# Later transposes of the rotated heads and the merged tiles, and gate rows summed over partitions as two float32r products

## The chip, the cores and the metric

The kernel runs on one core of a Trainium2 chip. The metric is device time in microseconds of one execution; of several executions the median is given. The engines are named as in the profile: PE (TensorE), DVE (VectorE), ACT (ScalarE), POOL (GpSimd) and SP (SyncE, which here only issues weight loads).

## The reference, cut to what matters

One layer of a decoder trunk, 256 tokens, width 2048. A conditioning vector `c` gives six modulation rows (shift, scale and gate, twice). The mixer projects the modulated input to linear-attention heads, sparse-attention heads with a partial rotary, an indexer and two merge gates; both branches are projected, gated, summed and projected again. The channel part is a SwiGLU.

```python
mod = jax.nn.silu(c) @ w_ada[layer] + b_ada[layer]
sh1, sc1, g1, sh2, sc2, g2 = [m[:, None, :] for m in jnp.split(mod, N_MOD, axis=-1)]
h = rms_norm(x, norm1_gain[layer]) * (1.0 + sc1) + sh1
x = x + g1 * hybrid_mixer(h, ...)
h = rms_norm(x, norm2_gain[layer]) * (1.0 + sc2) + sh2
x = x + g2 * swiglu(h, w_gate_up, w_down)
...
q_b = partial_rope(d_q.reshape(B, S, DSA_HEADS, DSA_HEAD_DIM), positions)
k_b = partial_rope(d_k.reshape(B, S, DSA_HEADS, DSA_HEAD_DIM), positions)
...
merged = jax.nn.sigmoid(gate_a) * y_a + jax.nn.sigmoid(gate_b) * y_b
return merged @ w_merge_out
```

The change touches how `q_b`, `k_b` and `merged` are turned so that their channels lie on partitions, and how the two gate rows `g1` and `g2` are summed.

## The kernel before

**The main stream.** Every large product is a list of chunks (`Mm`). A chunk is four rows of 128 weights by 512 columns. ACT rounds the weights to float32r (`hi`, line 311), DVE subtracts (`lo`, line 313), and PE makes three products for each of four rows and each half of the tokens (lines 351 to 353): 24 products of 128x512 per chunk, without a pause between chunks unless something waits. `hi` and `lo` have four buffers of half a chunk each, so ACT can round the halves of chunk i+2 only as PE is done with the halves of chunk i; `run()` (line 368) writes the program in that order: the products of chunk i, then the split of chunk i+2 (`pres`), then, at a group's last chunk, the group's evacuation, and then one step each of three side threads.

**Side threads.** `qa` (linear attention), `qb` (rotary, transposes, gate rows) and `qc` (indexer, sparse attention) are generators. One step's instructions stand between two chunks on PE, and behind the chunk's split on ACT and DVE. A step yields a cost; a thread steps only while the credit that chunks give lasts. `qb.drain` and `qc.drain` run steps at once where a result is needed. All engines are in-order, and the order is that in which the program is written.

**Rotated heads.** When a group of four heads is projected, `qk_evac` (line 926) copies it to `tm`, and `qk_transposes` (line 938) rotates it: `rope` puts six instructions on POOL (lines 784 to 789). Two empty steps later four transposes (line 949) go to PE, and ACT or DVE copies the result to `fA` or `fB` (line 951); a second half follows a step later. `attend(g)` (line 965) reads these at line 978.

**Merged tiles.** `y_b_evac` (line 1040) makes the merged tile `mm` with four DVE instructions (lines 1044 and 1045). `m_transposes` (line 1064) has one empty step, then two halves of four transposes (line 1055) with a cast on ACT (1060) and a subtraction on DVE (1061).

**Gate rows.** DVE gathers silu(c) times the weights per partition in `acc` (line 285). `reduce_rows` (line 902) sums `acc` over partitions: a float32 product of a matrix of ones with 512 columns of `acc`, and an addition on DVE. `g1_rows` (line 1130) does four such pieces, one per step, at the start of the merge projection; `g2_rows` (line 1264) at the start of the first down projection. `merge_evac(n)` and `down_evac(n)` first run `qb` until piece n is done.

**Buffers.** Small PE results rotate through three PSUM buffers `pa` (`psum_aux`), the main stream's through four, `pm`. The tile `tm` has one buffer.

Of the kernel before, what the change touches and what calls it, by code (L numbers as in the profile page):

```python
# [7 lines left out]
F32 = mybir.dt.float32  # L8
F32R = mybir.dt.float32r
I32 = mybir.dt.int32  # L10
AF = mybir.ActivationFunctionType
ALU = mybir.AluOpType
# [96 lines left out]
def tile_layer(tc, x, c, positions, norm1_gain, norm2_gain, w_ada, b_ada, w_in, gate_up, gate_bias,  # L109
               gla_gain, w_gla, w_dsa, w_merge, w_ffn_up, w_ffn_down, final_gain, cst, out):  # L110
    nc = tc.nc
    pe, act, dve, pool, sp = nc.tensor, nc.scalar, nc.vector, nc.gpsimd, nc.sync
    with (
# [11 lines left out]
        def name(s):  # L125
            serial[0] += 1
            return f"{s}_{serial[0]}"
# [4 lines left out]
        def psum_aux():  # L132
            return pp.tile([128, 512], F32, tag="pa", bufs=3, name=name("pa"))
# [7 lines left out]
        def parts8(tag):  # L141
            return g8(tag, F32R, (128, 8, S))
# [4 lines left out]
        def work(tag, bufs, shape, dt=F32):  # L147
            return wp.tile(list(shape), dt, tag=tag, bufs=bufs, name=name(tag))

        def t4(tag):  # L150
            return work(tag, 4 if tag == "mm" else 1, [128, 2, 512])
# [5 lines left out]
        cc = cp.tile([128, 528], F32, name="cc")  # L157
# [15 lines left out]
        posi = cp.tile([128, 2], I32, name="posi")  # L173
        act.dma_start(posi, positions.rearrange("(t p) -> p t", p=128), allow_slow_non_contiguous=True)

        ones = cp.tile([128, 128], F32, name="ones")
        pool.memset(ones, 1.0)
        half = cp.tile([128, 2], F32, name="half")
        pool.memset(half, -0.5)
        sc = cp.tile([128, 16], F32, name="sc")  # L180
# [595 lines left out]
        def rope(v, nh, dh, rot, step):  # L776

            hf = rot // 2
            vt = v.rearrange("p t (h e) -> p t h e", e=dh)
            a, b = vt[:, :, :, 0:hf], vt[:, :, :, hf:rot]  # L780
            co, si = (w[:, :, ::step].unsqueeze(2).to_broadcast([128, 2, nh, hf]) for w in (cos, sin))
            tmp = work("rp", 1, [128, 2, 128])
            u, w = (tmp[:, i, 0:2 * nh * hf].rearrange("p (t h e) -> p t h e", t=2, h=nh) for i in range(2))
            pool.tensor_tensor(u, a, si, ALU.mult)  # L784
            pool.tensor_tensor(w, b, si, ALU.mult)
            pool.tensor_tensor(a, a, co, ALU.mult)
            pool.tensor_tensor(a, a, w, ALU.subtract)
            pool.tensor_tensor(b, b, co, ALU.mult)
            pool.tensor_tensor(b, b, u, ALU.add)

        ikw = cp.tile([128, 2, 72], F32, name="ikw")
        bias = cp.tile([128, 384], F32, name="bias")
# [85 lines left out]
        accs = {}  # L878
# [20 lines left out]
            act.dma_start(t, row.unsqueeze(0).to_broadcast([128, D]))  # L899
            return t  # L900

        def reduce_rows(dst, n):

            o = slice(n * 512, (n + 1) * 512)
            ps = psum_aux()
            pe.matmul(ps, ones, accs["t"][:, o], start=True, stop=True)  # L906
            dve.tensor_tensor(dst[:, o], dst[:, o], ps, ALU.add)

        for i, seg in enumerate((4, 3, 2, 5)):
            for j in range(16):  # L910
# [15 lines left out]
        def qk_evac(which, g):  # L926
            def f(ps):
                qb.drain()
                tm = t4("tm")
                for t in range(2):  # L930
                    if which == 0:
                        act.mul(tm[:, t], ps[t], 128 ** -0.5)  # L932
                    else:
                        dve.tensor_copy(tm[:, t], ps[t])
                qb.add(qk_transposes(which, g, tm))
            return f

        def qk_transposes(which, g, tm):
            rope(tm, 4, 128, 32, 1)
            yield 0.2  # L940
            yield 0.2
            qc.drain(lambda: done_heads[0] >= g * 4)
            dst = t4("fB" if which else "fA").rearrange("p a b -> p (a b)")
            heads[g, which] = dst
            for i in range(2):
                ps = psum_aux()
                for a in range(2):
                    for t in range(2):
                        pe.transpose(ps[:, a * S + t * 128:a * S + t * 128 + 128],  # L949
                                     tm[:, t, (i * 2 + a) * 128:(i * 2 + a + 1) * 128], ident)  # L950
                (act.copy if i else dve.tensor_copy)(dst[:, i * 512:(i + 1) * 512], ps)
                yield 0.4
# [87 lines left out]
        def y_b_evac(n):  # L1040
            def f(ps):
                sg = state["sg"]
                for t in range(2):
                    dve.tensor_tensor(sg[:, t], sg[:, t], ps[t], ALU.mult)
                    dve.tensor_tensor(mm[n][:, t], mm[n][:, t], sg[:, t], ALU.add)
                qb.add(m_transposes(n))
            return f

        def split_transposes(src, kt0, dst):

            for i in range(2):
                ps = psum_aux()
                for a in range(2):
                    for t in range(2):
                        pe.transpose(ps[:, a * S + t * 128:a * S + t * 128 + 128],  # L1055
                                     src[:, t, (i * 2 + a) * 128:(i * 2 + a + 1) * 128], ident)
                kt = kt0 + i * 2
                hi = dst[kt // 8][:, kt % 8:kt % 8 + 2, :].rearrange("p a t -> p (a t)")
                lo = dst[2 + kt // 8][:, kt % 8:kt % 8 + 2, :].rearrange("p a t -> p (a t)")
                act.copy(hi, ps)  # L1060
                dve.tensor_sub(lo, ps, hi.bitcast(F32))
                yield 0.7

        def m_transposes(n):
            if n == 0:
                for i in range(4):
                    mT[i] = parts8("gA" if i < 2 else "gB")
            yield
            for cost in split_transposes(mm[n], n * 4, mT):
                state["mT"] = state.get("mT", 0) + 2  # L1070
                yield cost
# [17 lines left out]
        late = {}  # L1089

        def merge_start():
            for t in range(2):
                x1[t] = g8(("gC", "gD")[t])
                act.dma_start(x1[t], x[t * 128:(t + 1) * 128, :])
            late["h2"] = hpair()
            late["g1"] = bcast_row("gr", b_ada[2 * D:3 * D])
            late["g1_done"] = 0
            qb.add(g1_rows())
# [29 lines left out]
            qn.step()  # L1128

        def g1_rows():  # L1130
            for n in range(4):
                reduce_rows(late["g1"], n)
                late["g1_done"] = n + 1
                yield 0.7

        def need_m(kt, t):
            if kt >= 12:
# [124 lines left out]
            act.dma_start(late["fg"], final_gain.unsqueeze(0).to_broadcast([128, D]))  # L1262

        def g2_rows():
            for n in range(4):
                reduce_rows(late["g2"], n)
                late["g2_done"] = n + 1
                yield 0.7

        def down_token(n, t, ps, last):  # L1270
            c = slice(n * 512, (n + 1) * 512)
# [40 lines left out]
        for p, (g0, ng) in enumerate(FF_PARTS):  # L1312
            ex = spread(0) if p == 0 else None
            at_first = len(items)
            for n in range(ng):
                if p == 0 and n == 1:
                    items.append(Call(g2_start))
                for which in range(2):
                    add_group(w_ffn_up, which * DFF + (g0 + n) * 512, 512,
                              Grp(act_h2, up_evac(which, n, n * 4), need_h2), extra=ex if n else None)  # L1320
            if p == 0:
                by_token(at_first)
                items[at_first].ahead = AHEAD - 1
                items[at_first].home = (lambda: g8("gr", F32R), free_acc)
                items.append(Call(lambda: qb.add(g2_rows())))

            def need(kt, t, k0=g0 * 4, top=ng * 4 - 4):
                if kt - k0 >= top:
                    qb.drain(lambda: late["ready"] > kt - k0)
            for n in range(4):  # L1330
                add_group(w_ffn_down, n * 512, 512,
                          Grp(lambda kt, k0=g0 * 4: act_ff(kt - k0), down_evac(n, p == 2), need), g0 * 4, ng * 4)
# [45 lines left out]
```

## Time and profile before

| | |
|---|---|
| median of 3 runs | 1880.08 us (1878.12 to 1884.08) |
| the profiled execution | 1886.39 us, its span 1883.5 us |
| PE busy | 1834.3 us, 97% of the span |
| DVE, ACT, POOL busy | 1286.3, 852.2, 115.8 us |
| the chain that ended last | 88% PE, 84% in lines 351 to 353 |
| mean granted TensorE clock | 0.993 of full |

The trace's rows are read as follows: a start in microseconds from the span's start, a duration, the engine, the line, what is written and read, a count where rows are merged, and in brackets how long the engine had been idle and what ended that. A PE product is pipelined: its row is longer than the distance to the next one's start, so costs on PE are read from starts.

### The profile page before, as it was taken

The numbers are of one execution on the slowest core, as the hardware profiler recorded it, in microseconds if no ns is written. First come the engines' busy times: TensorE is split into PE (matmuls) and PEld (weight loads), VectorE is DVE, ScalarE is ACT, GpSimd is POOL, SyncE is SP. The second block draws the span as 40 slices with busy tenths as digits, with TensorE's granted clock in tenths as the row PEclk, the third lists the DMA queues.
The fourth block names the chain that finished last, engine by engine and source line by source line (L and its number), as shares of the span: only waits on it lengthen the run. The fifth ranks groups of instructions, "written<-read, shape, count | busy, mean of one in ns | idle before, by whom it ended". The sixth has DMA issues, their size and how long they took to land.

```text
span 1883.5 us, 23110 instructions
## 1 busy us (share of the span) xinstructions
PE 1834.3 (97%) x9132; PEld 1508.9 (80%) x9132; DVE 1286.3 (68%) x1441; ACT 852.2 (45%) x1114; POOL 115.8 (6%) x141
## 2 busy tenths in 40 slices
PE   3999999999999999999999999999999999999998
PEld 3888888877788888788887787888788888888886
DVE  6899875898765678777777656677555544554455
ACT  4554444655645444344433446444334444334443
POOL 0000000533210000200000000000000000000002
PEclk8999999999999999999999999999999999999999
DMA  9999853644455888878888754899565555555553
GB/s 369 386 348 317 282 158 105 201 136 153 139 162 172 280 301 291 289 254 293 312 304 309 270 197 160 324 323 314 179 200 193 187 191 188 190 191 195 185 180 133
DMA packets 198077, 440.89 MB, mean 234 GB/s; under 512 B 7832, under 2 KB 14128, under 8 KB 188880
## 3 DMA queue, kind: packets, MB, share of 16 engines
q1 hardware_dynamic: 196544, 433.69, 67.1%
q10 hardware_dynamic: 1424, 5.72, 0.8%
q8 instruction: 71, 1.16, 0.2%
q14 instruction: 38, 0.31, 0.0%
HBM read 437.29 MB, written 2.10 MB: 233 GB/s over the span
## 4 chain that ended last, share of the span: by engine, by line
PE 88%; DVE 5%; DMA 2%; issue 2%; ACT 2%; POOL 1%; SPq 0%; ACTq 0%; POOLq 0%; DVEq 0%
PE pm L351 28%; PE pm L352 28%; PE pm L353 28%; DVE lo L313 2%; DVE acc L285 1%; DMA raw<-in_w_in_dram 1%; ACT hi L311 1%; PE pa L1055 1%; DMA raw<-in_w_branch_dsa_dram 1%; PE pa L978 0%; DVE acc L679 0%; PE pa L949 0%; PE pa L1001 0%; DMA raw<-in_w_ada_dram 0%; PE pa L906 0%
## 5 line engine op out<-in xcount | busy, mean ns | idle before, releaser
L313 DVE TENSOR_TENSOR lo<-raw,hi 128x1024 fp32r<-128x1024 f32 (+1 forms) x630 | 764.8, 1225 | 527.8 <-ACT hi L311 527.3
L311 ACT CAST hi<-raw 128x1024 fp32r<-128x1024 f32 (+1 forms) x630 | 650.4, 1043 | 899.7 <-PE pm L353 690.8
L351 PE MATMUL pm<-hi,h 128*128 128x512 f32 (+1 forms) x1784 | 699.4, 392 | 2.2 <-ACT h L470 1.9
L353 PE MATMUL pm<-hi,h 128*128 128x512 f32 (+1 forms) x1784 | 690.7, 387 | 0.0
L352 PE MATMUL pm<-lo,h 128*128 128x512 f32 (+1 forms) x1784 | 690.2, 387 | 0.2 <-DVE lo L313 0.2
L351 PEld LDWEIGHTS pm<-hi,h 128*128 128x128 f32 x1784 | 336.2, 188 | 70.7 <-ACT h L470 2.3
L353 PEld LDWEIGHTS pm<-hi,h 128*128 128x128 f32 x1784 | 335.9, 188 | 68.8 <-DVE h L477 0.2
L352 PEld LDWEIGHTS pm<-lo,h 128*128 128x128 f32 x1784 | 336.2, 188 | 66.3 <-DVE lo L313 0.7
L351 PE MATMUL pm<-hi,gA 128*128 128x512 f32 x608 | 241.9, 398 | 0.0
L352 PE MATMUL pm<-lo,gA 128*128 128x512 f32 x608 | 236.8, 389 | 0.2 <-DVE lo L313 0.2
L353 PE MATMUL pm<-hi,gB 128*128 128x512 f32 x608 | 236.9, 390 | 0.0
L285 DVE SCALAR_TENSOR_TENSOR acc<-raw,sc,acc 128x2048 f32<-128x2048 f32 (+2 forms) x122 | 218.2, 1790 | 7.6 <-DMA raw<-in_w_ada_dram 6.7
L352 PEld LDWEIGHTS pm<-lo,gA 128*128 128x128 f32 x608 | 114.2, 188 | 25.5 <-issue 1.4
L351 PEld LDWEIGHTS pm<-hi,gA 128*128 128x128 f32 x608 | 114.2, 188 | 24.8 <-issue 1.9
L353 PEld LDWEIGHTS pm<-hi,gB 128*128 128x128 f32 x608 | 114.1, 188 | 23.7
L1279 POOL TENSOR_TENSOR gC<-gC,gr 128x512 f32<-128x512 f32 x3 | 4.9, 1647 | 716.6 <-ACT pm L1277 716.6
L670 POOL TENSOR_TENSOR acc<-gC 128x512 f32<-128x512 f32 x32 | 39.2, 1235 | 38.5 <-DVE acc L679 38.1
L679 DVE TENSOR_TENSOR acc<-gB,acc 128x256 f32<-128x256 f32 x64 | 31.2, 548 | 6.9 <-ACT acc L674 6.8
L986 ACT ACTIVATE S<-S,mx 128x128 f32<-128x128 f32 (+1 forms) x32 | 14.3, 448 | 32.8 <-DVE mx L984 32.8
L784 POOL TENSOR_TENSOR rp<-tm,sin 128x128 f32<-128x128 f32 x9 | 8.3, 921 | 308.6 <-ACT tm L932 183.8
L674 ACT ACTIVATE acc<-acc 128x256 f32<-128x256 f32 x64 | 22.2, 415 | 6.9 <-POOL acc L670 6.7
L351 PE MATMUL pm<-hi,gr 128*128 128x512 f32 x64 | 24.9, 389 | 0.0
(271 smaller groups left out, 1041.3 us busy)
## 6 DMA issues: line engine op xcount, KB each, us to landing
raw<-in_w_in_dram SPq DMA_DIRECT2D x129, 1024.0 KB, 5.1
raw<-in_w_ffn_gate_up_dram SPq DMA_DIRECT2D x88, 1024.0 KB, 5.1
raw<-in_w_ada_dram SPq DMA_DIRECT2D x64, 1024.0 KB, 5.0
raw<-in_w_ffn_down_dram SPq DMA_DIRECT2D x44, 1024.0 KB, 5.1
raw<-in_w_ada_dram SPq DMA_DIRECT2D x64, 512.0 KB, 8.6
raw<-in_w_branch_gla_dram SPq DMA_DIRECT2D x16, 1024.0 KB, 5.2
raw<-in_w_branch_dsa_dram SPq DMA_DIRECT2D x16, 1024.0 KB, 5.2
raw<-in_w_merge_out_dram SPq DMA_DIRECT2D x16, 1024.0 KB, 5.3
```

Of the source, the lines that this page charges most:

```text
L285: dve.scalar_tensor_tensor(a[:, g], it.raw[:, j, g], s, a[:, g], ALU.mult, ALU.add)
L311: act.copy(hv, src)
L313: rests.append(lambda lv=lv, src=src, hv=hv: dve.tensor_sub(lv, src, hv.bitcast(F32)))
L351: pe.matmul(o, a, hv, start=it.first and k == 0, stop=False)
L352: pe.matmul(o, a, lv, start=False, stop=False)
L353: pe.matmul(o, b, hv, start=False, stop=it.last and k == it.nk - 1)
L670: pool.tensor_tensor(d, v, v[:, :, s - 1:s].to_broadcast([128, n, 2 * s]), ALU.subtract)
L674: act.activation(d, d, AF.Exp, scale=(1.0 if u else -1.0) / 16)
L679: dve.tensor_tensor(w, src, d, ALU.mult)
L784: pool.tensor_tensor(u, a, si, ALU.mult)
L986: act.activation(nst[:, a:b], nst[:, a:b], AF.Exp, bias=mx[:, t:t + 1], accum_out=sm[:, t:t + 1])
L1055: pe.transpose(ps[:, a * S + t * 128:a * S + t * 128 + 128], src[:, t, (i * 2 + a) * 128:(i * 2 + a + 1) * 128], ident)
```

## The change

1. `qk_transposes` has a third empty step, `m_transposes` a second one. The transposes of every rotated group and of every merged tile stand one chunk later on PE.
2. `reduce_rows` becomes a generator over the four pieces. For each piece ACT rounds 512 columns of `acc` to float32r (`hv`) and DVE subtracts (`lv`), into the single buffer of `tm`; a step later PE multiplies ones with `hv` and with `lv`, and DVE adds the sum. The rounding of the next piece stands in the same step behind that addition.
3. `ones` becomes float32r, written at the start by an ACT activation (0 times the constants plus 1) that stands ahead of the activation that makes silu(c); POOL's memset goes.

```diff
-        ones = cp.tile([128, 128], F32, name="ones")
-        pool.memset(ones, 1.0)
+        ones = cp.tile([128, 128], F32R, name="ones")
+        act.activation(ones, cc[:, 0:128], AF.Identity, bias=1.0, scale=0.0)
...
-        def reduce_rows(dst, n):
-
-            o = slice(n * 512, (n + 1) * 512)
-            ps = psum_aux()
-            pe.matmul(ps, ones, accs["t"][:, o], start=True, stop=True)
-            dve.tensor_tensor(dst[:, o], dst[:, o], ps, ALU.add)
+        def reduce_rows(dst, done):
+
+            for n in range(4):
+                o = slice(n * 512, (n + 1) * 512)
+                both = work("tm", 1, [128, 2, 512], F32R)
+                hv, lv = both[:, 0], both[:, 1]
+                act.copy(hv, accs["t"][:, o])
+                dve.tensor_sub(lv, accs["t"][:, o], hv.bitcast(F32))
+                yield 0.7
+                ps = psum_aux()
+                pe.matmul(ps, ones, hv, start=True, stop=False)
+                pe.matmul(ps, ones, lv, start=False, stop=True)
+                dve.tensor_tensor(dst[:, o], dst[:, o], ps, ALU.add)
+                late[done] = n + 1
...
             rope(tm, 4, 128, 32, 1)
             yield 0.2
             yield 0.2
+            yield 0.1
             qc.drain(lambda: done_heads[0] >= g * 4)
...
             yield
+            yield
             for cost in split_transposes(mm[n], n * 4, mT):
...
         def g1_rows():
-            for n in range(4):
-                reduce_rows(late["g1"], n)
-                late["g1_done"] = n + 1
-                yield 0.7
+            yield from reduce_rows(late["g1"], "g1_done")
...
         def g2_rows():
-            for n in range(4):
-                reduce_rows(late["g2"], n)
-                late["g2_done"] = n + 1
-                yield 0.7
+            yield from reduce_rows(late["g2"], "g2_done")
```

Three places show how instructions move. The first is PE at the transposes of the last rotated keys (`tm_6616`, group 3). Before, they stand ahead of the chunk whose first weights are `hi_6653`:

```order
L353 MATMUL pm_6627<-hi_6608,h_105 128x512
L949 MATMUL pa_6700<-cc,tm_6616 128x128 x4
L351 MATMUL pm_6626<-hi_6653,h_105 128x512
L352 MATMUL pm_6626<-lo_6654,h_105 128x512
L353 MATMUL pm_6626<-hi_6653,h_105 128x512
```

With the change they stand behind that chunk:

```order
L351 MATMUL pm_6627<-hi_6657,h_105 128x512
L352 MATMUL pm_6627<-lo_6658,h_105 128x512
L353 MATMUL pm_6627<-hi_6657,h_105 128x512
L958 MATMUL pa_6737<-cc,tm_6616 128x128 x4
L351 MATMUL pm_6626<-hi_6689,h_105 128x512
```

So 24 products have come between the copy to `tm_6616` and its transposes.

The second place is PE at the end of the linear attention: the last two tiles of its output are turned (line 760), and the first logits of the sparse attention follow (line 978; 987 with the change). Before, from the second half of the first keys' transposes (`pa_4944`) on:

```order
L949 MATMUL pa_4944<-cc,tm_4763 128x128 x4
...
L760 MATMUL pa_4987<-cc,gr_111 128x128
...
L760 MATMUL pa_4996<-cc,gr_111 128x128
...
L978 MATMUL pa_5006<-fB_4885,fA_4668 128x128
L978 MATMUL pa_5006<-fB_4885,fA_4668 128x256
L351 MATMUL pm_5017<-hi_4916,h_105 128x512
```

With the change:

```order
L760 MATMUL pa_4981<-cc,gr_111 128x128
...
L760 MATMUL pa_4990<-cc,gr_111 128x128
...
L958 MATMUL pa_4999<-cc,tm_4763 128x128 x4
L987 MATMUL pa_5006<-fB_4937,fA_4716 128x128
L987 MATMUL pa_5006<-fB_4937,fA_4716 128x256
L351 MATMUL pm_5017<-hi_4909,h_105 128x512
```

Four `pa` tiles now stand between two chunks, where three did; `pa_5006` takes the buffer of `pa_4981`, where it took that of `pa_4944`, used a chunk earlier.

The third place is the start of the merge projection, on PE and DVE. Before, the first piece of the row stands on PE between the third and the fourth chunk of the group (and each further piece behind one more chunk):

```order
L353 MATMUL pm_8460<-hi_8489,gB_7486 128x512
L906 MATMUL pa_8577<-acc_7538,ones 128x512
L351 MATMUL pm_8459<-hi_8526,gA_7484 128x512
L352 MATMUL pm_8459<-lo_8527,gA_7484 128x512
L353 MATMUL pm_8459<-hi_8526,gB_7486 128x512
```

With the change, on PE, behind the group's fourth chunk:

```order
L353 MATMUL pm_8460<-hi_8523,gB_7486 128x512
L912 MATMUL pa_8614<-tm_8611,ones 128x512
L913 MATMUL pa_8614<-tm_8611,ones 128x512
L912 MATMUL pa_8628<-tm_8618,ones 128x512
L913 MATMUL pa_8628<-tm_8618,ones 128x512
L351 MATMUL pm_8635<-hi_8560,gA_7483 128x512
```

and on DVE, from the split of the chunk after next on:

```order
L313 TENSOR_TENSOR lo_8606<-raw_8493,hi_8605 128x1024
L909 TENSOR_TENSOR tm_8611<-acc_7538,tm_8611 128x512
L914 TENSOR_TENSOR gr_8457<-gr_8457,pa_8614 128x512
L909 TENSOR_TENSOR tm_8618<-acc_7538,tm_8618 128x512
L1116 TENSOR_TENSOR fC_8621<-gr_8457,pm_8459 128x512
```

The first two pieces stand back to back, a chunk later than the first one did: the evacuation of group 0 needs piece 0, and the ordinary step behind it brings piece 1. On ACT the roundings `tm_8611` and `tm_8618` stand one behind the other, behind the rounding of `hi_8605`. At the down projection the same pair stands on PE behind the fourth chunk, but there the rounding of piece 0 stands a chunk ahead of its products; that of piece 1 stands as here.

## Rows read from the trace of the kernel before

**Rows 1.** The page's first part: busy time of each engine, its share of the span, its instructions.

```profile
PE 1834.3 (97%) x9132; PEld 1508.9 (80%) x9132; DVE 1286.3 (68%) x1441; ACT 852.2 (45%) x1114; POOL 115.8 (6%) x141
```

**Rows 2.** The waits of PE over the whole span: who was waited for, then total us, times, the longest.

```profile
PE pa L949 <- POOL tm L789: 3.8, 1, 3.8
PE pa L1161 <- DVE mm L1156: 2.2, 4, 0.9
...
PE pa L1055 <- DVE mm L1045: 1.6, 2, 0.9
```

**Rows 3.** The timeline of PE around the transposes of the last rotated keys, and around their second half. Between the rows of 797.67 and 802.94 stand 12 more products, one start behind the other.

```profile
792.68 0.39 PE L353 MATMUL pm<-hi,h 128*128 128x512 f32 x1
796.91 1.12 PE L949 MATMUL pa<-cc,tm 128*128 128x128 f32 x4 [3.84 <-POOL tm L789]
797.67 0.78 PE L351 MATMUL pm<-hi,h 128*128 128x512 f32 x1
...
802.51 0.63 PE L353 MATMUL pm<-hi,h 128*128 128x512 f32 x1
802.94 0.44 PE L351 MATMUL pm<-hi,h 128*128 128x512 f32 x1
...
805.74 0.60 PE L949 MATMUL pa<-cc,tm 128*128 128x128 f32 x4
...
806.41 0.39 PE L352 MATMUL pm<-lo,h 128*128 128x512 f32 x1
```

**Rows 4.** The timeline of POOL: the last instruction of that group's rotary.

```profile
796.40 0.45 POOL L789 TENSOR_TENSOR tm<-tm,rp 128x128 f32<-128x128 f32 x1
```

**Rows 5.** Two stretches by windows: PE busy (instructions), PEld, DVE, ACT, POOL, then the granted clock, the busy share of the DMA engines and GB/s.

```profile
800.00:802.00 2.00, 2.00 (x6) 1.61 (x5) 1.01 (x1) 0.00 (x0) 0.00 (x0) 0.50 0.06 25
1138.00:1142.00 4.00, 2.31 (x12) 1.43 (x11) 2.82 (x5) 1.77 (x4) 0.82 (x2) 1.00 0.54 208
```

**Rows 6.** The timeline of PE: the transposes of one merged tile that wait.

```profile
1002.71 0.30 PE L1055 MATMUL pa<-cc,mm 128*128 128x128 f32 x1 [0.64 <-DVE mm L1045]
1003.94 0.55 PE L1055 MATMUL pa<-cc,mm 128*128 128x128 f32 x3 [0.93 <-DVE mm L1045]
```

**Rows 7.** The timeline of PE: a piece of a gate row (line 906; a float32 product is two instructions) between products of the main stream.

```profile
1060.01 0.40 PE L353 MATMUL pm<-hi,gB 128*128 128x512 f32 x1
1060.24 1.02 PE L906 MATMUL pa<-acc,ones 128*128 128x512 f32 x2
...
1061.33 0.40 PE L352 MATMUL pm<-lo,gA 128*128 128x512 f32 x1
```

**Rows 8.** The timelines of ACT (the first two rows and the fourth), PE (the third) and DVE (the rest): ACT's order behind a split, and the end of the merge projection's first group.

```profile
1054.52 1.05 ACT L311 CAST hi<-raw 128x1024 fp32r<-128x1024 f32 x1 [1.67 <-PE pm L353]
1055.47 0.58 ACT L1060 CAST gA<-pa 128x512 fp32r<-128x512 f32 x1
...
1066.33 0.40 PE L353 MATMUL pm<-hi,gB 128*128 128x512 f32 x1
1066.76 1.05 ACT L311 CAST hi<-raw 128x1024 fp32r<-128x1024 f32 x1 [1.67 <-PE pm L353]
1067.84 1.22 DVE L313 TENSOR_TENSOR lo<-raw,hi 128x1024 fp32r<-128x1024 f32 x1 [1.50 <-ACT hi L311]
1068.98 0.68 DVE L1106 TENSOR_TENSOR fC<-gr,pm 128x512 f32<-128x512 f32 x1
1069.70 0.69 DVE L1107 TENSOR_TENSOR gC<-gC,fC 128x512 f32<-128x512 f32 x1
```

**Rows 9.** Lines 1060 and 1061 by themselves: count, then duration in ns (least, median, most).

```profile
L1060 ACT CAST gA<-pa x30: 572/580/586, 913.6 to 1820.2; 128x512 fp32r<-128x512 f32 x30
...
L1061 DVE TENSOR_TENSOR gB<-pa,gA x30: 682/684/684, 917.6 to 1821.5; 128x512 fp32r<-128x512 f32 x30
```

**Rows 10.** The timelines of PE, ACT and DVE where the last output of the linear attention is turned and the first logits follow (line 765 casts a `pa` tile's halves on ACT, line 766 subtracts on DVE; two tiles, so four of each).

```profile
566.91 1.04 PE L760 MATMUL pa<-cc,gr 128*128 128x128 f32 x8
567.79 0.82 PE L978 MATMUL pa<-fB,fA 128*128 128x128 f32 x4
...
568.60 0.48 ACT L765 ACTIVATE gA<-pa,cols 128x256 fp32r<-128x256 f32 x1
...
570.00 0.47 DVE L766 SCALAR_TENSOR_TENSOR gB<-pa,cols,gA 128x256 fp32r<-128x256 f32 x1
570.51 0.84 ACT L765 ACTIVATE gA<-pa,cols 128x256 fp32r<-128x256 f32 x2 [1.43 <-DVE gB L766]
571.01 0.88 DVE L766 SCALAR_TENSOR_TENSOR gB<-pa,cols,gA 128x256 fp32r<-128x256 f32 x2 [0.54 <-ACT gA L765]
```

**Rows 11.** The timelines of PE and of its weight loads: five `pa` tiles between two chunks, four of column sums (line 487, each read by one DVE instruction) and one of a merged tile.

```profile
910.93 2.04 PE L487 MATMUL pa<-cc,acc 128*128 128x128 f32 x16
...
912.91 0.42 PEld L1055 LDWEIGHTS pa<-cc,mm 128*128 128x128 f32 x4 [0.18 <-DVE mods L488]
```

**Rows 12.** The timelines of ACT, DVE and PE at the start.

```profile
4.12 1.28 ACT L181 ACT_TABLE_LOAD   x1 [4.12 <-DMA cc<-in_constants_dram]
...
6.66 0.60 ACT L451 ACTIVATE pm<-gB 128x512 f32<-128x512 f32 x1 [1.03 <-DMA gB<-in_x_dram]
...
12.70 0.75 DVE L283 TENSOR_SCALAR acc<-raw,sc 128x1024 f32<-128x1024 f32 x1 [4.72 <-DMA raw<-in_w_ada_dram]
...
33.31 1.08 PE L487 MATMUL pa<-cc,acc 128*128 128x128 f32 x4 [10.35 <-DVE acc L285]
```

## The prediction

> **What bounds the kernel now.** I read the page's busy times first: PE is busy 97% of the span, DVE 68%, ACT 45% [rows 1]. So time comes only from PE: from products it need not make, from waits, and from its clock. Next PE's waits [rows 2]: apart from the start and the second norm (line 1161), which the change leaves alone, the transposes of rotated heads wait once, 3.8 us, and those of merged tiles 1.6 us in two pieces. Then the timeline around the long wait [rows 3]: the products before it start 0.23 us apart; after it the clock is at half [rows 5] (0.50 of full in 800 to 802, so 1.2 GHz), and thirteen products take 5.27 us (797.67 to 802.94), 0.41 us each. After waits of at most 0.9 us in the norm the granted clock is 1.00 (2.4 GHz) [rows 2, 5]. What PE did before the fall is plain: it stood still for 3.84 us.
>
> **What the later transposes remove.** The rotary of the last keys ends at 796.85 on POOL [rows 4]. With the change one chunk stands ahead of the transposes: 24 products of 0.227 us, 5.45 us. The last product before them started at 792.68, so PE reaches them at 792.91 + 5.45 = 798.4, 1.5 us after POOL is done: no wait. If POOL were 1.5 us later the cover would be gone and each further us would cost one. The price of the wait with its clock: four transposes at full clock take 806.41 - 0.23 - 805.74 = 0.44 us [rows 3], thirteen products 2.95, so the fourteenth product would start at 792.91 + 3.39 = 796.30; it starts at 802.94. That is 6.6 us, 4.0 of wait and 2.6 of half clock. The weights do not come late instead: in 800 to 802 the DMA engines were 6% busy [rows 5]: nothing was late. The waits of the merged tiles' transposes, 0.64 + 0.93 [rows 6], go too, since the DVE sums are done a chunk later: 1.6 us. **Removed: 8.2 us.**
>
> **What the float32r rows save by themselves.** A piece takes PE from 1060.24 to 1061.33 - 0.23 = 1061.10, 0.86 us [rows 7]. Two float32r products of 512 columns take 2 x 0.227 = 0.45. Eight pieces: 8 x 0.41 = **3.3 us** saved. Eight roundings on ACT (0.58 us) and eight subtractions on DVE (0.68) [rows 9] have room there as such [rows 1]; their place is the question.
>
> **The new waits: pieces 0 and 1 of g1.** In the order, piece 0's rounding stands behind that of `hi_8605`, which waits for PE to leave the group's last chunk, and its products are the next thing on PE. The last product starts at 1066.33 and the chunk ends at 1066.56; call that 0. ACT starts the half-chunk rounding at 0.20 and DVE its subtraction at 1.28 [rows 8]. ACT's next instruction starts 0.95 behind such a rounding (1054.52 to 1055.47), at 1.15, and with 0.58 ends at 1.73; the first product can run. DVE's next starts at 2.42 (1068.98) and ends at 3.10; the second product runs, and ends its slot at 3.35. Another engine sees that 0.20 later (as ACT did above), 3.55. Now piece 1: `tm` has one buffer, so only now does ACT round (to 4.13), while DVE makes the addition; DVE's following instruction starts some 0.66 behind it (0.72 and 0.61 lie between such ones), at 4.2, and ends at 4.9. The last product ends at 5.15. Four products are 0.9 of this, so PE waits **4.2 us**, in pieces of 1.7, 1.1, 0.6 and 0.8. Queued behind it are the next group's products on PE, the merge's residual on DVE, the next roundings on ACT; ACT and DVE have a chunk of PE time to recover, so pieces 2 and 3 do not wait.
>
> **g2.** Piece 0 is prepared a chunk ahead and costs no wait. Piece 1 needs ACT at 1.15 to 1.73 and DVE, which first makes the split (to 2.42) and the addition of piece 0 (0.66), from 3.1 to 3.75; the last product ends at 4.0. Less four products: **3.1 us**.
>
> **The first logits.** With a fourth `pa` tile between two chunks, `pa_5006` needs the buffer of `pa_4981`, whose second half is read last by the second of the four instructions of line 766. Before, that one runs in the pair at 571.01, to about 571.45, because ACT and DVE first split weights and copy values and then alternate over each tile's halves [rows 10]. PE is through its twelve transposes at about 567.79 + 0.44 = 568.2. So it would wait to 571.5: **3.3 us**. The nearest row in which a buffer is reused between the same two chunks is cheap: 0.18 us before the merged tile's transposes [rows 11], where each tile has one reader at the head of DVE's queue. Here four readers and two splits stand ahead, so I take 3.3 and keep 0.2 as the lower end. The Trainium skill speaks against the edit: its page Perfetto Trace Analysis, section Matmuls, says that independent matmul groups should rotate through different PSUM banks, so that the evacuation of one overlaps the next one's products. By that sentence the whole evacuation shows, some 3 us; by the wait of 0.18 us the sum would be 3.1 us lower.
>
> **Costs taken at nothing.** The copies behind the moved transposes only change places on ACT and DVE. The last group's transposes before the merge now stand directly ahead of the chunk that reads them, but its second half reads the late pair: DVE ends that subtraction at about 2.42 + 0.68 = 3.1 behind the chunk before [rows 8, 9], and PE needs it some 3.7 behind (0.44 of transposes, half a chunk of 2.7, two products of 0.45); without that 0.6 of cover, it would cost what is missing. At the start, a table load of 1.28 us and a short activation go ahead of silu(c), which then ends near 7.2 instead of 5.6; DVE needs it at 12.70, when its weights come. The squares of x move from 6.66 by the same half us, which ends in PE's wait of 10.35 us for DVE's column sums [rows 12].
>
> **The sum.** Removed 8.2 + 3.3 = 11.5; added 4.2 + 3.1 + 3.3 = 10.6: -0.9 us. There remains the clock. One fall costs 2.6 us, by the one seen after 3.84 us; none follows waits up to 0.9. The new waits lie between: 3.3 in one piece, 3.1 in two, 4.2 in four. I give one of the three a fall as likeliest: **+1.7 us**. The profiled execution took 1886.39 us, 6.3 above the median; a difference of places carries over, so I put it on the median: 1880.08 + 1.7, about **1882 us**. About 0.3%, 5.6 us, is what can be told from no change.
>
> **The rivals.**
> - *Forecast: gains and new waits cancel*, with no, one or two falls of the clock: -0.9, +1.7 or +4.3, so 1879 to 1884.5. Chance 0.76.
> - *Slower: the clock falls at all three new waits.* Then +6.9, 1887 us. It decides if waits in pieces, with single products between them, count like the whole one of 3.84 us. For it speaks that the wait of 3.3 us is close to 3.84; against it that pieces of up to 0.9 us left the clock alone. Chance 0.12.
> - *Faster: the new waits hardly show*, at 0.2 us each as in [rows 11]: -11.5 + 0.6, about 1869; half of them shown gives about 1874.5. For it speaks only that reuse was cheap once; against it that PE, ACT and DVE run in order, and that the rounding cannot start before PE leaves the last chunk. Chance 0.07.
> - *The later place does not do what it says*: the rotary ends later by what the transposes move, so that the wait and its half clock stay. Then -0.9 + 6.6, and 1886 to 1888 with a fall. Against it, POOL waits for nothing on PE. Chance 0.05.
>
> **Chances and range.** Faster by over 0.3%: 0.07; within 0.3%: 0.76; slower: 0.17 (the second and the fourth case). The range goes from 1875 (the first logits' wait at its lower end, no fall) to 1887 (all three fall), and leaves out the full gain and the worst of the fourth case.
>
> **What would show it.** Right: in PE's waits no line of the rotary's transposes and none of the merged tile's; instead the first logits waiting for line 766 near 568, some 3 us; the ones products waiting for ACT and DVE near 1060 and 1345, some 4 and 3 us; pairs of products of 0.45 us per piece; the granted clock at half after one of these. Wrong: a ones product waiting under 1 us, a rotary wait that stays, or a PE wait at the fourth merge chunk.

## The result and the profile after

The changed kernel takes 1889.95 us (median of 6 runs, 1888.69 to 1891.92); the kernel before, beside it on the same chip, 1880.07 (6 runs, 1877.30 to 1884.08). The ratio is 1.0054 (95% interval 1.0040 to 1.0067): slower by 0.54%, some 10 us. The forecast was 1882 and its range ended at 1887, so the time lies outside it, on the slower side.

The profiled execution of the changed kernel took 1889.6 us, its span is 1887.8. The page's first part, to be laid beside [rows 1], shows nothing of it:

```profile
PE 1835.4 (97%) x9132; PEld 1510.7 (80%) x9132; DVE 1292.3 (68%) x1449; ACT 857.7 (45%) x1124; POOL 115.9 (6%) x140
```

PE's instructions are as many as before (eight float32 products of two instructions each have become sixteen float32r products), and its busy time is 1 us more. What changed is found in the waits of PE, the view of [rows 2] (total us, times, the longest):

```profile
PE pa L912 <- ACT tm L908: 3.5, 3, 1.7
PE pa L987 <- DVE gB L766: 3.3, 1, 3.3
PE pa L913 <- DVE tm L909: 2.5, 3, 1.4
PE pa L1168 <- DVE mm L1163: 2.2, 4, 0.9
```

The rotary's transposes (now line 958) and the merged tiles' (now line 1064) stand in this view no more. In their place are the three waits that the prediction named: the logits (line 987) for the second half of a copied tile, and the ones products (lines 912 and 913) for ACT's rounding and DVE's subtraction. Line 1168, the second norm, is as before. The words "the first logits" in the prediction mean the logits of the second group of heads, `attend(1)`, which follow at once on the last output of the linear attention.

The timeline of PE after shows the places one after another: the logits, the rotary, pieces 0 and 1 of `g1`, pieces 0 and 1 of `g2`.

```profile
567.53 0.60 PE L958 MATMUL pa<-cc,tm 128*128 128x128 f32 x4
571.39 0.89 PE L987 MATMUL pa<-fB,fA 128*128 128x128 f32 x4 [3.25 <-DVE gB L766]
571.93 0.58 PE L351 MATMUL pm<-hi,h 128*128 128x512 f32 x1
...
575.67 0.48 PE L351 MATMUL pm<-hi,h 128*128 128x512 f32 x1
576.00 0.39 PE L352 MATMUL pm<-lo,h 128*128 128x512 f32 x1
...
803.67 0.60 PE L958 MATMUL pa<-cc,tm 128*128 128x128 f32 x4
...
1061.77 0.39 PE L353 MATMUL pm<-hi,gB 128*128 128x512 f32 x1
1063.82 0.50 PE L912 MATMUL pa<-tm,ones 128*128 128x512 f32 x1 [1.65 <-ACT tm L908]
1065.15 0.49 PE L913 MATMUL pa<-tm,ones 128*128 128x512 f32 x1 [0.84 <-DVE tm L909]
1066.36 0.50 PE L912 MATMUL pa<-tm,ones 128*128 128x512 f32 x1 [0.71 <-ACT tm L908]
1067.08 0.56 PE L913 MATMUL pa<-tm,ones 128*128 128x512 f32 x1 [0.23 <-DVE tm L909]
1067.45 0.63 PE L351 MATMUL pm<-hi,gA 128*128 128x512 f32 x1
...
1070.83 0.40 PE L353 MATMUL pm<-hi,gB 128*128 128x512 f32 x1
...
1342.41 0.39 PE L912 MATMUL pa<-tm,ones 128*128 128x512 f32 x1
1342.64 0.40 PE L913 MATMUL pa<-tm,ones 128*128 128x512 f32 x1
1344.23 0.50 PE L912 MATMUL pa<-tm,ones 128*128 128x512 f32 x1 [1.19 <-ACT tm L908]
1346.16 0.50 PE L913 MATMUL pa<-tm,ones 128*128 128x512 f32 x1 [1.44 <-DVE tm L909]
1346.51 0.40 PE L351 MATMUL pm<-hi,gA 128*128 128x512 f32 x1
```

The sizes are those of the prediction. The logits wait 3.25 us (3.3 was said). In `g1` the last product before the pieces ends its slot at 1061.77 + 0.23 = 1062.00 and the first one behind them starts at 1067.45: 5.45 us, less 0.9 for four products, is 4.5 (4.2 was said). In `g2` it is 1346.51 - 1342.41 = 4.1, less 0.9, 3.2 (3.1 was said). At the rotary (803.67) nothing waits.

The rows also show what the forecast did not count on. After each of the three waits the products start further apart. Ten starts between 571.93 and 575.67 lie 0.43 or 0.34 us apart instead of 0.23; by the sum over them 1.80 us are lost there, by the same sum 1.57 us from 1067.45 to 1070.43, and 1.61 from 1347.2 to 1350.6. The windows of these stretches, and of the one of [rows 5] (columns as there):

```profile
574.00:576.00 2.00, 2.00 (x7) 1.59 (x5) 0.00 (x0) 0.47 (x2) 0.00 (x0) 0.54 0.00 0
800.00:802.00 2.00, 2.00 (x10) 1.65 (x9) 2.00 (x2) 0.00 (x0) 0.00 (x0) 1.00 0.83 292
1068.00:1070.00 2.00, 2.00 (x6) 1.52 (x5) 1.97 (x4) 1.01 (x3) 0.00 (x0) 0.50 0.52 197
1348.00:1350.00 2.00, 2.00 (x6) 1.60 (x5) 1.93 (x4) 0.00 (x0) 0.00 (x0) 0.50 0.69 268
```

The granted clock is at half (1.2 GHz) behind all three waits, and at full where [rows 5] had it at half. PE stood still for 3.25 us ahead of the first fall; ahead of the others it was idle in pieces of at most 1.65 and 1.44 us, with single products between.

That `g1` goes as worked out is seen in ACT and DVE (timelines after; the first three rows are ACT's, the rest DVE's):

```profile
1062.20 1.04 ACT L311 CAST hi<-raw 128x1024 fp32r<-128x1024 f32 x1 [1.67 <-PE pm L353]
1063.15 0.61 ACT L908 CAST tm<-acc 128x512 fp32r<-128x512 f32 x1
1065.69 0.62 ACT L908 CAST tm<-acc 128x512 fp32r<-128x512 f32 x1 [1.92 <-PE pa L913]
...
1063.27 1.23 DVE L313 TENSOR_TENSOR lo<-raw,hi 128x1024 fp32r<-128x1024 f32 x1 [1.49 <-ACT hi L311]
1064.42 0.68 DVE L909 TENSOR_TENSOR tm<-acc,tm 128x512 fp32r<-128x512 f32 x1
1065.69 0.69 DVE L914 TENSOR_TENSOR gr<-gr,pa 128x512 f32<-128x512 f32 x1 [0.59 <-PE pa L913]
1066.34 0.69 DVE L909 TENSOR_TENSOR tm<-acc,tm 128x512 fp32r<-128x512 f32 x1
```

The half-chunk split of the weights stands ahead of piece 0's rounding on both engines, and the rounding of piece 1 waits (1.92 us) until PE has read the single `tm`.

### The profile page after: what moved, and what is told of

Same layout as the page of the kernel before. It is cut to its first block, busy times and chain, and to the rows that moved or that the text cites. A ratio compares the mean times of both kernels' runs of the same rounds, so it can differ in the third digit from the quotient of the medians.

```text
span 1887.8 us, 23128 instructions
## 1 busy us (share of the span) xinstructions
PE 1835.4 (97%) x9132; PEld 1510.7 (80%) x9132; DVE 1292.3 (68%) x1449; ACT 857.7 (45%) x1124; POOL 115.9 (6%) x140
## 4 chain that ended last, share of the span: by engine, by line
PE 91%; DVE 4%; ACT 2%; issue 2%; DMA 1%; POOL 0%; SPq 0%; ACTq 0%; POOLq 0%; DVEq 0%
PE pm L351 29%; PE pm L353 29%; PE pm L352 29%; DVE acc L285 1%; DVE lo L313 1%; ACT hi L311 1%; PE pa L1064 1%; DVE acc L679 1%; PE pa L987 1%; PE pa L1010 0%; DMA raw<-in_w_ada_dram 0%; PE pa L487 0%; PE ph L686 0%; PE pa L958 0%; DMA gB<-in_x_dram 0%
```

## The experiments

Ten runs were made, of eight new kernels and once more of each of the two, all beside runs of the kernel before on the same chip; the ratios are to those. Two theories were set down first. **A:** the kernel before ordinarily doesn't wait at the rotary as its profiled execution did (that one stood 6.3 us above the median), so the later transposes have little to give. **B:** the wait is there, and the difference lies in the new waits, each with its own fall of the clock, as the prediction's slower rival has it.

**The kernel before once more** (no edit), with a profile of an execution nearer to the median.

> The kernel before, unchanged, to see another execution of it. Theory A (the rotary's wait of 3.84 us with its half clock, 6.6 us together, belonged to the one execution that was profiled, which took 1886.4 us, and not to the ordinary ones at 1880): the median is again near 1880, and if the profiled execution takes about 1880 us, PE has no wait, or one under 1.5 us, for the rotary of the last keys near 797. Rival B (the wait is in every execution, and the 6 us between the profile and the median lie elsewhere): the wait of 3 to 4 us with half clock is there again.

Measured: 1882.16 us, ratio 0.9999 (0.9989 to 1.0008); its profiled execution took 1882.98. The timeline of PE and two windows at the rotary, the views of [rows 3, 5]:

```profile
797.59 1.08 PE L949 MATMUL pa<-cc,tm 128*128 128x128 f32 x4 [3.65 <-POOL tm L789]
798.32 0.78 PE L351 MATMUL pm<-hi,h 128*128 128x512 f32 x1
```

```profile
798.00:800.00 2.00, 2.00 (x8) 1.71 (x7) 1.30 (x2) 0.00 (x0) 0.00 (x0) 0.50 1.05 407
800.00:802.00 2.00, 2.00 (x8) 1.54 (x8) 1.65 (x1) 0.00 (x0) 0.00 (x0) 0.73 0.40 168
```

The wait is there again, 3.65 us against 3.84, so A does not hold for this execution. But the half clock ends within the window of 800 to 802, at about 801.1, and costs 1.00 us by the sum over the products, where the execution of [rows 3] lost 2.25 by the same sum. The merged tiles' wait of [rows 6] is not there at all. Laid product by product over the execution shown ahead of the prediction, this one gains 1.4 us at the rotary's half clock and 1.9 at the merged tile: 2.9 at the end with all small steps. So the wait is not peculiar to the first execution, and the price that the prediction read from it was too high. Whether ordinary executions all have the wait is taken up again at the rows prepared ahead.

**The later heads alone.**

```diff
             yield 0.2
+            yield 0.1
             qc.drain(lambda: done_heads[0] >= g * 4)
```

> Only the rotated heads' transposes one chunk later. Theory A: nothing is removed in an ordinary execution; the logits of group 1 wait 3.3 us near 570 for the reused buffer and the clock falls behind that for 1.8 us: +5 us, 1885. Rival B: the rotary's 6.6 us go, +5.1 come: -1.5 us, 1878.5.

Measured: 1882.93 us, ratio 1.0006 (0.9997 to 1.0015). The logits' wait comes with this edit alone (timeline of PE, and the window behind it):

```profile
570.77 1.35 PE L979 MATMUL pa<-fB,fA 128*128 128x128 f32 x4 [3.25 <-DVE gB L766]
```

```profile
572.00:574.00 2.00, 2.00 (x6) 1.59 (x5) 1.21 (x4) 0.93 (x5) 0.00 (x0) 0.50 0.43 168
```

Here the half clock lost 1.00 us. The rotary's wait is gone, so much of what the edit takes away near 797 it puts back near 571. The time lies between A's 1885 and B's 1878.5 and decides for neither.

**The later merged tiles alone.**

```diff
             yield
+            yield
             for cost in split_transposes(mm[n], n * 4, mT):
```

> Only the merged tiles' transposes one chunk later. Both theories: the 1.6 us of waits near 1003 go and nothing comes, since the two float32 pieces that now stand back to back need no preparation: -1.6 us, 1878.5; in A as in B the rotary stays as it is.

Measured: 1880.88 us, ratio 0.9997 (0.9987 to 1.0007), where both theories had 1878.5. The merged wait is not there, the rotary's is (3.28 us). No gain can be told from none, which agrees with a wait that some executions don't have.

**The float32r rows alone**, with one empty step ahead of the merged transposes, as before.

```diff
-            ps = psum_aux()
-            pe.matmul(ps, ones, accs["t"][:, o], start=True, stop=True)
...
+                act.copy(hv, accs["t"][:, o])
+                dve.tensor_sub(lv, accs["t"][:, o], hv.bitcast(F32))
+                yield 0.7
+                ps = psum_aux()
+                pe.matmul(ps, ones, hv, start=True, stop=False)
+                pe.matmul(ps, ones, lv, start=False, stop=True)
...
```

> Only the float32r rows. Without the later merged transposes the first piece of g1 is prepared a chunk ahead, as that of g2 is. Both theories: 3.3 us less product time, two waits of 3.2 us (near 1062 and 1345) and two falls of the clock of 1.6 us: +6.3 us, 1886.5. If the clock did not fall, +3.1.

Measured: 1886.66 us, ratio 1.0026 (1.0016 to 1.0036), 5.3 above the kernel before beside it (1881.33, 35 runs). The profiled execution is the slowest of the twelve (1890.74). The rotary's wait is still there (3.5 us). Of the windows, that behind the `g1` pieces and that behind `g2`'s:

```profile
1068.00:1070.00 2.00, 2.00 (x6) 1.51 (x6) 1.30 (x3) 1.23 (x3) 0.00 (x0) 0.50 0.60 229
...
1348.00:1350.00 2.00, 2.00 (x8) 1.55 (x7) 1.97 (x4) 0.49 (x1) 0.00 (x0) 0.64 1.02 395
```

The edit that takes 3.1 us of products away makes the kernel slower: its waits (at `g1` and at `g2` 1.19 and 1.44 us each) eat that, and two falls of the clock, 2.60 and 1.58 us, come on top. (A third stands behind the second norm near 1144; it is taken up in the next part.) At `g1` only piece 1 waits here. In the whole change piece 0 waits too, since the merged tiles' later transposes push it into the step just ahead of its products: the two edits disturb each other.

**The rows prepared ahead.** To take the waits away and keep the products, each piece is split two steps ahead, alternately into `tm` and the idle `fA`.

```diff
+                both = work(("tm", "fA")[n % 2], 1, [128, 2, 512], F32R)
...
+            split(0)
+            split(1)
+            yield 0.7
+            for n in range(4):
...
+                if n < 2:
+                    split(n + 2)
+                yield 0.7
```

Both generators are advanced to their first `yield` before they are queued.

> Only the float32r rows, but with two buffers (that of tm and that of fA, free by then), the first two pieces split before the transposes ahead of them and each further one two steps ahead. Waiting theory: the ones products find their halves ready, no wait near 1062 and 1345, no fall of the clock there: eight pieces of 0.41 us less, -3.3 us, 1878. Rival (the two products or their splits cost by themselves, or the clock falls for what PE does there): the falls of 1.6 to 2.6 us stay, near 1881 or above.

Measured: 1877.56 us, ratio 0.9983 (0.9974 to 0.9991). A piece now costs the path two products and no wait (timeline of PE, first piece of `g1`; [rows 7] has the same piece before):

```profile
1060.16 0.40 PE L353 MATMUL pm<-hi,gB 128*128 128x512 f32 x1
1060.39 0.39 PE L919 MATMUL pa<-fA,ones 128*128 128x512 f32 x1
1060.62 0.39 PE L920 MATMUL pa<-fA,ones 128*128 128x512 f32 x1
1060.86 0.40 PE L351 MATMUL pm<-hi,gA 128*128 128x512 f32 x1
```

From 1060.39 to 1060.86 are 0.47 us, 0.39 less than the 0.86 of [rows 7]. The clock stays at full behind both groups of pieces. So the same products with the same rounding cost +0.26% or give -0.17%, and the wait for their preparation is what decides.

The same profile, of the median run, brings A back in part. Between the first chunk and the merge projection nothing is changed here, and yet the rotary's wait is short and no half clock follows it (timeline of PE, window behind, timeline of POOL):

```profile
794.03 0.66 PE L967 MATMUL pa<-cc,tm 128*128 128x128 f32 x4 [1.37 <-POOL tm L789]
```

```profile
794.00:796.00 2.00, 1.97 (x11) 1.71 (x12) 2.00 (x3) 0.00 (x0) 0.00 (x0) 1.00 0.87 337
```

```profile
793.53 0.45 POOL L789 TENSOR_TENSOR tm<-tm,rp 128x128 f32<-128x128 f32 x1
```

Laid over the second profile of the kernel before, this execution gains 3.9 us at the rotary alone. The merged tiles' wait is here (1.5 us).

**The later heads, but not for group 1**, in the kernel before and in the changed one. This leaves group 1's transposes where they were, so that the logits find a free buffer.

```diff
-            yield 0.1
+            if g != 1:
+                yield 0.1
```

> Rotated heads' transposes one chunk later except for group 1, whose keys' second half met the end of the linear attention. Waiting theory: no wait for line 766 near 570 and none for the rotary near 797: -5 us (3.7 of wait, 1.0 to 2.5 of clock), 1876. Rival (the wait near 570 has to do with the copies to fB and not with the reused buffer, or another wait takes the rotary's place): no better than the 1883 of the later heads alone.

Measured: 1877.80 us, ratio 0.9985 (0.9977 to 0.9994). The expectation was 1876. There is no wait near 570, the logits run beside the transposes as in [rows 10], and none at the rotary. But the rotary's cover is thin (timelines of POOL, DVE and PE):

```profile
795.33 2.39 POOL L789 TENSOR_TENSOR tm<-tm,rp 128x128 f32<-128x128 f32 x1
...
794.86 2.55 DVE L285 SCALAR_TENSOR_TENSOR acc<-raw,sc,acc 128x2048 f32<-128x2048 f32 x1
...
797.78 0.66 PE L951 MATMUL pa<-cc,tm 128*128 128x128 f32 x4
```

POOL ends at 797.72 and PE starts at 797.78.

> The whole change, but group 1's heads in their old place. Waiting theory: against the changed kernel (1890) the wait of 3.25 us near 570 and its half clock of 1.8 go: 1885; the waits of the rows stay. Rival as for the version before: 1890.

Measured: 1886.17 us, ratio 1.0028 (1.0019 to 1.0038): with the logits' wait gone, the changed kernel is still slower, and what is left are the rows. The same edit is thus worth 3.7 to 3.8 us: each kernel taken against the one before beside it, +9.88 less +6.14 in the changed kernel, and +1.60 less -2.23 for the later heads alone. This run also holds the one new wait that no fall followed, at `g2` (timeline and windows):

```profile
1339.98 0.50 PE L912 MATMUL pa<-tm,ones 128*128 128x512 f32 x1 [1.19 <-ACT tm L908]
1341.92 0.50 PE L913 MATMUL pa<-tm,ones 128*128 128x512 f32 x1 [1.44 <-DVE tm L909]
```

```profile
1342.00:1344.00 2.00, 2.00 (x9) 1.65 (x10) 1.93 (x4) 0.62 (x1) 0.00 (x0) 1.00 0.81 283
1344.00:1346.00 2.00, 2.00 (x11) 1.64 (x10) 1.71 (x3) 0.78 (x1) 0.00 (x0) 1.00 0.57 219
```

The waits are the same 1.19 and 1.44 us as in the changed kernel.

**All three edits, mended:** later heads but for group 1, later merged tiles, rows prepared ahead (the diffs above together).

> The whole change with both mends: group 1's heads in their old place, rows split ahead into two buffers. Waiting theory: -5 (heads) -3.3 (rows) and 0 to -1.6 (merged tiles): -8 to -10 us, 1872, with no wait of PE left between 480 and 1130 above 0.5 us. Rival (gains of this kind are given back elsewhere, by weights that come later): 1878 or more.

Measured: 1873.84 us (5 runs, 1873.28 to 1874.18), ratio 0.9965 (0.9952 to 0.9979). It beats both kernels. The waits of PE hold none of the new ones, and the rotary's transposes wait 0.38 us for POOL.

**The mended kernel without the later merged tiles** (the second `yield` of `m_transposes` taken out again), and **the changed kernel once more**.

> The version with both mends, but the merged tiles' transposes in the old place, for the worth of that edit alone among runs that scatter little. If the wait of 0.5 to 1.6 us for the merged tile is in most executions: 1874.5 to 1875.5 against 1873.8. If it is chance (it was missing in one profile of the kernel before): the same 1873.8.

Measured: 1875.16 us (1873.16 to 1876.44), ratio 0.9963 (0.9950 to 0.9975), where all three edits had 0.9965 (0.9952 to 0.9979), on another chip. The intervals reach some 2.5 us to either side, so the merged edit's worth stays unsettled. This profile has no wait for a merged tile although its transposes stand in the old place.

> The changed kernel, unchanged, in another execution and with more runs. Waiting theory, with the clock as seen so far (it fell at seven of eight of the new waits): waits of 3.3, 3.6 (beside its products) and 2.6 us at the same places, again two or three falls of 1.0 to 2.6 us, 1887 to 1891. Rival (the falls in the first profile were chance, and something unseen makes the time): fewer than two falls and still 1890.

Measured: 1889.63 us, ratio 1.0040 (1.0026 to 1.0053). The same three waits (PE's view has 3.5 us for line 912, 3.3 for 987, 2.3 for 913), and again three falls, of 1.29, 1.00 and 1.61 us. The rotary's transposes wait 0.32 us for POOL here.

## Why the prediction was off

**What held.** PE bounds the kernel. The rotary's wait (but for 0.32 us in the second profile) and the merged tiles' go. A float32r piece saves 0.39 us (0.41 was said). The three new waits stand where they were said to, with the engines that were named, and measure 3.25, 4.5 and 3.2 us against 3.3, 4.2 and 3.1. At the logits it was right to work the wait out from the readers of the older buffer and not to take the 0.18 us of [rows 11]; the Trainium skill, page Perfetto Trace Analysis, section Matmuls, on rotating through PSUM banks so that one group's evacuation overlaps the next one's products, is agreed with by these 3.25 us, and by their absence where one tile fewer stands in the rotation. The costs taken at nothing (the copies, the start, the last merged transposes) show no wait.

**The step that failed: "I give one of the three a fall as likeliest."** All three had one, in both profiles of the changed kernel, and over all kernels 10 of the 11 new waits (2.6 to 3.4 us of idle time each); so had all four rotary waits of 3.3 to 3.8 us, while the one of 1.37 us had none. Pieces of 1.65, 0.84, 0.71 and 0.23 us with single products between them were followed by half clock like a whole wait of 3.25. The sum counted 2.6 us of clock; there were 1.80 + 1.57 + 1.61 = 5.0, 2.4 more. This is the rival of the slower side, which had a chance of 0.12. The price of one fall was wrong the other way: 1.0 to 1.9 us behind nine of these ten waits, 2.6 behind one.

What spoke against the falls in the prediction, that pieces of up to 0.9 us in the norm left the clock alone, was drawn from one execution, and from a window that ends at 1142.00, just behind the second of the norm's two longest waits. In that execution the clock did stay at full, as in most. But in two of the twelve profiles, those of the later heads but for group 1 and of the float32r rows alone, half clock followed the same norm waits. The first of them (timeline of PE, and a window):

```profile
1131.04 0.66 PE L1163 MATMUL pa<-cc,mm 128*128 128x128 f32 x4 [0.82 <-DVE mm L1158]
1132.57 0.66 PE L1163 MATMUL pa<-cc,mm 128*128 128x128 f32 x4 [0.87 <-DVE mm L1158]
```

```profile
1134.00:1136.00 2.00, 2.00 (x7) 1.58 (x7) 2.00 (x6) 0.95 (x2) 0.00 (x0) 0.50 0.00 0
```

So in these two executions half clock followed pieces of at most 0.88 us; in the other ten the same waits were not followed by it.

**The second error: one execution's gain, put on the median of all.** "A difference of places carries over" did not hold, because the places removed were themselves dearer in the profiled execution than in others: the rotary's half clock (2.25 us by the sum over the products, against 1.00, 1.19 and 0.80 in three other kernels that have this wait) and the merged wait (1.6 us, and none in the second profile of the same kernel; of seven profiles with these transposes in the old place three have none). That execution stood 6.3 us above the median, and part of that was what the change took away. By medians the later heads gave 2.2 us where they brought no logits' wait with them, where the prediction took 6.6 for the rotary. This error counts as much as the clock: with all three falls the prediction's own sum ends at 1887, still 3 us short.

**Slips in the working.** Between the rows of 797.67 and 802.94 stand 11 products, not 12, so twelve products take the 5.27 us; by the prediction's own way the rotary's price is then 6.9 us, not 6.6. The lower end of the range, with the logits' wait at 0.2 us, comes to 1876 and not 1875. Neither bears on the miss.

**How the difference adds up.** The starts of the same main products, relative to the first, in the changed kernel less those in the second profile of the kernel before:

| place | us |
|---|---|
| the first chunk | +0.6 |
| the logits: wait and clock | +3.93 + 1.66 = +5.6 |
| the rotary: wait and clock | -4.42 - 1.40 = -5.8 |
| `g1`, pieces 0 and 1: waits and clock, less what they save | +4.58 + 1.18 = +5.8 |
| `g2`, pieces 0 and 1: the same | -0.46 + 3.23 + 1.25 = +4.0 |
| four further pieces | 4 x -0.39 = -1.6 |
| a dozen moved transposes and small steps, none over 0.6 | -0.7 |
| at the last product | +7.9 |

The first product itself starts 1.07 us earlier in the changed kernel (37.01 against 38.08), so the spans differ by 6.8. Against the execution shown ahead of the prediction the same difference is +5.0, which is the prediction's -0.9 with the three falls' 5.0, and some 0.9 of small steps. So of the 8.2 us between forecast (+1.7) and measured medians (+9.9) about 3.3 are in the sum, most of it clock; 2.9 are the dear execution; the remaining 2.0 are not accounted for and lie within the scatter of the kernel before, whose runs span 7 us. Executions with the short rotary wait of 1.37 us could hold them; how many of the runs without a profile have it is not known.

**A cover that was not as said.** The prediction had PE reach the rotary's transposes 1.5 us after POOL is done. It was 4.2 us in the first profile of the changed kernel (POOL ended at 798.99 + 0.46 = 799.45, PE came at 803.67), 0.06 us in the later heads but for group 1, and less than nothing in the second profile of the changed kernel and with all edits mended, where PE waits 0.32 and 0.38 us. The logits' wait is not what makes the cover, since the second profile has it too. What differs is POOL's last rotary instruction (line 789): 0.45 us in [rows 4] and 0.46 in the first profile of the changed kernel, where DVE does nothing beside it, and 2.39 where DVE's line 285 stands beside it for 2.07 us, as in the rows of the later heads but for group 1. In all twelve profiles the instructions of lines 788 and 789 fall into two sorts: 160 of 0.45 to 0.65 us, and 80 of 1.32 to 2.39, every one of which has at least 1.0 us of DVE's weight work (lines 285 and 313) beside it. That speaks for DVE as the cause; no run tried it. The prediction took POOL's end from one execution, as it took the wait.

**What stays open.** What decides whether half clock follows a wait of about 3 us, and for how long: the same `g2` waits were followed by 1.61 us of loss in one kernel and by none in another, and the norm's by half clock in two profiles of twelve. How often an ordinary execution of the kernel before has the long rotary wait. And what the merged tiles' edit is worth by itself.

## What to carry to other kernels

Where PE is the bound, a new wait of some 3 us is to be priced with a fall of the clock behind it, also when single products break it up; and a fix counts only by what the wait costs in more than one execution, above all when the profiled one is above the median. Before PE work is moved, count the tiles of its PSUM rotation between the same two chunks, and see that what its operands need is written a full step ahead into a buffer that nobody still reads: with both (group 1's heads left in their place, the rows split two steps ahead) the three edits went from 0.54% slower to 0.35% faster.

## What the runs showed of the hardware

A wait and the loss behind it vary from one execution to another: at the rotary, in kernels that leave its transposes in the old place, four profiles have 3.28 to 3.84 us of wait and lost 0.80 to 2.25 us to half clock, and a fifth has 1.37 us and lost none. A POOL instruction of 128x128 took 0.45 us with DVE idle and 2.39 with a DVE instruction over 128x2048 beside it. The runs of the kernel before spread over 1876.95 to 1884.70 us (35 runs on one chip), the 5 of the kernel with all edits mended over 1873.28 to 1874.18; but 5 without the later merged tiles spread over 3.3 us, so it is not shown that the scatter went with the waits.
